# Four channel blocks at a time in the first modulation of a hybrid diffusion layer: weights in 512-channel packets

## The chip, the core and the metric

The kernel runs on one core of one Trainium2 chip. The metric is device time in microseconds (us) of one execution; the median of three executions stands for the kernel, and the range of the three is shown with it. TensorE multiplies matrices; VectorE, ScalarE and GpSimd do elementwise work; SyncE issues most of the transfers from device memory. The profile calls the engines PE (with PEld for its weight loads), DVE, ACT, POOL and SP.

## The reference, cut to what matters

One layer over 512 latent tokens and 256 context tokens, 1024 channels. The part that the change touches is the first of the two adaptive norms:

```python
mod_x = (jax.nn.silu(c) @ w_ada[l] + b_ada[l]).reshape(bsz, N_MOD, 1, D_MODEL)
mod_c = (jax.nn.silu(c_ctx) @ w_ada[l] + b_ada[l]).reshape(N_MOD, D_MODEL)
hc = rms_norm(ctx, norm1_w[l]) * (1.0 + mod_c[1]) + mod_c[0]
hx = rms_norm(x, norm1_w[l]) * (1.0 + mod_x[:, 1]) + mod_x[:, 0]
zs = hn @ w_in[:, :N_STATE_COLS]      # hn is hc, then hx; and so on for the layer
```

Here `mod[0]` is the shift and `mod[1]` the scale, each 1024 channels, and each channel needs a sum over the 1024 entries of `silu(c)`. Everything behind it (two token mixers, their merge, the gated MLP with a 3x3 convolution, the last norm) is unchanged.

## The kernel before

Products keep nearly full float32 precision by splitting each factor into a rounded part ("hi", type fp32r) and a rest ("lo"): `mm3` makes hi·hi, hi·lo and lo·hi. ScalarE makes the hi part with a cast, VectorE or GpSimd the lo part with a subtraction. The order in which each engine's instructions stand is set when the program is built, by a scheduler that places the instructions of the written program by its own reckoning of their times; on the chip each engine then works its list from the top and waits where an operand is not there yet.

The stage in question is `streams`, the first of the kernel. It runs like this:

- `stream_load` brings the six 128-token blocks (two of context, four of latents) as `xn`, 128 x 1024. `stream_in` takes the root mean square (a square on ScalarE, `rpow` with a power on GpSimd), scales `xn` on VectorE, transposes eight 128 x 128 squares on TensorE (`ps_xt`) and copies them to `xT`, half on ScalarE, half on VectorE. So channels lie on partitions.
- `ada_load(k, j)` brings the weights of one block k of 128 channels, for shift (j = 0) or scale (j = 1): 16 tiles `uw`, each 1024 input rows by 128 channels, 512 KB. They share nine buffers with the `xn`.
- `ada_rows(k)` multiplies them: the conditioning vectors (four columns: hi and lo of latent and context) are the stationary operand, the weights the moving one. The six tiles in `UF` go as plain float32, eight products of 128 columns each; the other ten are split into `uh` (ScalarE, two buffers) and `ul` (VectorE, two buffers), sixteen products of 128 columns each. ScalarE copies the four rows out as `adr`.
- `ada_cols(k)` transposes the rows back to channels on partitions (two small transposes), adds bias and parts (`adt`, `mod`) and forms `modA`, the scale of block k.
- `stream_mod(k)` applies `modA` and `modB` to block k of `xT`: `hx` and `hc` (hi, on ScalarE), `hl_t` (VectorE), and the lo parts on VectorE (latents) and GpSimd (context).
- `products(k)` adds block k to four sums: `ps_gc` and `ps_gx` (the gates' weights `wg`) and `pc_k` and `px_k` (the first head's key weights `wk0`), twelve products. Later the first head's `px_q` and `pc_v` follow in the same way.

The loop over k calls `ada_cols(k)`, `stream_mod(k)`, `products(k - 1)` and `ada_rows(k + 2)`: each block of 128 channels has its own small chain from its two weight tiles to its products. The weights `wk0`, `wq0`, `wv0` of the projections are split by `split`, whose subtraction runs on GpSimd in this stage (`sub_eng`).

Of the kernel before, what the change touches and what calls it, by code (L numbers as in the profile page):

```python
# [66 lines left out]
class Kern:  # L67
# [175 lines left out]
        self.modA = cp.tile([P, KC, 2], F32, tag="modA", name="modA")  # L243
        self.modB = self.mod[:, 0:8, :]

    def ada_load(self, k, j, xp):
# [4 lines left out]
        return w

    def ada_rows(self, k, ap):

# [1 line left out]
        ps = self.pt([P, 512], ("mg", "po")[k % 2], f"ps_ada{k}")
        for j in range(2):
            w = self.uw[2 * k + j]
            if (2 * k + j) in UF:
                for i in range(KC):  # L260
                    nc.tensor.matmul(ps[0:4, P * j : P * j + P], self.sc4[:, i, :], w[:, i, :], start=i == 0, stop=i == KC - 1)
                continue
            hi = ap.tile([P, KC, P], F32R, tag="uh", name=f"uh{k}_{j}", bufs=UH)
            lo = ap.tile([P, KC, P], F32R, tag="ul", name=f"ul{k}_{j}", bufs=UH)
# [2 lines left out]
            for p in (hi, lo):
                for i in range(KC):
                    nc.tensor.matmul(ps[0:4, P * j : P * j + P], self.sch[:, i, :], p[:, i, :], start=i == 0 and p is hi, stop=i == KC - 1 and p is lo)
        r = ap.tile([4, 2 * P], F32, tag="adr", name=f"adr{k}", bufs=2)  # L270
        nc.scalar.copy(r, ps[0:4, 0 : 2 * P])
        return ps, r

    def ada_cols(self, k, ps, r, ap):

        nc = self.nc
        for j in range(2):
            nc.tensor.transpose(ps[:, 256 + 4 * j : 260 + 4 * j], r[:, P * j : P * j + P], self.ident[0:4, 0:4])
        t = ap.tile([P, 2, 4], F32, tag="adt", name=f"adt{k}", bufs=2)
        nc.vector.tensor_tensor(t, ps[:, 256:264].rearrange("p (n j) -> p n j", j=4),  # L280
                                self.bada4[:, k : 16 : KC, :], ALU.add)
        m = self.mod[:, k : 16 : KC, :]
        nc.vector.tensor_tensor(m, t[:, :, 0:2], t[:, :, 2:4], ALU.add)
        nc.vector.scalar_tensor_tensor(self.modA[:, k, :], self.mod[:, KC + k, :], 1.0, self.n1w[:, k : k + 1].broadcast_to([P, 2]), ALU.add, ALU.mult)
# [1349 lines left out]
```

## Time and profile before

| | |
|---|---|
| median of 3 runs | 1322.67 us (1321.39 to 1322.98) |
| the profiled execution, its own time | 1323.87 us |
| its span, first to last instruction | 1322.2 us |
| TensorE busy | 1284.0 us, 97% of the span |
| VectorE busy | 888.1 us, 67% |
| ScalarE busy | 585.0 us, 44% |
| GpSimd busy | 531.3 us, 40% |
| mean granted TensorE clock | 0.993 |

All durations below come from the one profiled execution. Its own time is 1.67 us above its span and 1.2 us above the median. A "busy" TensorE counts modelled ends of pipelined products, so what a product costs in a dense run is read from the distance between the starts of neighbours. The stage of the change is the first 70 us of the span.

### The profile page before, as it was taken

The numbers are of one execution on the slowest core, as the hardware profiler recorded it, in microseconds if no ns is written. First come the engines' busy times: TensorE is split into PE (matmuls) and PEld (weight loads), VectorE is DVE, ScalarE is ACT, GpSimd is POOL, SyncE is SP. The second block draws the span as 40 slices with busy tenths as digits, with TensorE's granted clock in tenths as the row PEclk, the third lists the DMA queues.
The fourth block names the chain that finished last, engine by engine and source line by source line (L and its number), as shares of the span: only waits on it lengthen the run. The fifth ranks groups of instructions, "written<-read, shape, count | busy, mean of one in ns | idle before, by whom it ended". The sixth has DMA issues, their size and how long they took to land.

```text
span 1322.2 us, 24197 instructions
## 1 busy us (share of the span) xinstructions
PE 1284.0 (97%) x9454; PEld 1089.1 (82%) x9454; DVE 888.1 (67%) x1809; ACT 585.0 (44%) x1283; POOL 531.3 (40%) x679
## 2 busy tenths in 40 slices
PE   6998899999999999999999999999999999999997
PEld 4886778888888888998899888888788888888886
DVE  6877777857857757253745585444679879887843
ACT  5565664666655744233333354222344333333322
POOL 4313330123122238486847550000445545555542
PEclk9999899999999999999999999999999999999999
DMA  9634233232332244454524433438233333333231
GB/s 282 157 107 117 53 90 101 77 80 77 80 96 68 71 103 134 107 153 107 136 72 128 120 86 92 140 96 253 65 118 90 96 95 98 97 104 98 67 108 68
DMA packets 233248, 141.86 MB, mean 107 GB/s; under 512 B 32992, under 2 KB 215533, under 8 KB 233133
## 3 DMA queue, kind: packets, MB, share of 16 engines
q1 hardware_dynamic: 230973, 140.09, 37.9%
q8 instruction: 74, 1.21, 0.4%
q10 hardware_dynamic: 2160, 0.23, 0.1%
q14 instruction: 41, 0.34, 0.1%
HBM read 134.47 MB, written 5.82 MB: 106 GB/s over the span
## 4 chain that ended last, share of the span: by engine, by line
PE 77%; DVE 6%; ACT 2%; DMA 2%; issue 1%; SPq 0%; POOL 0%; POOLq 0%; ACTq 0%; DVEq 0%
PE pu L124 12%; PE pd L124 6%; PE pu L125 6%; PE py L124 4%; PE px_g L124 4%; PE pv L124 3%; PE pd L125 3%; PE py L125 2%; PE px_g L125 2%; PE px_mo L124 2%; PE po L986 2%; PE pv L125 2%; PE p L1003 2%; PE px_q L124 1%; PE px_z L124 1%; PE px_v L124 1%
## 5 line engine op out<-in xcount | busy, mean ns | idle before, releaser
L1604 DVE SCALAR_TENSOR_TENSOR y<-pu,fw,y 128x441 f32<-128x441 f32 (+2 forms) x352 | 230.0, 690 | 41.1 <-ACT y L1595 35.4
L299 POOL TENSOR_TENSOR aw<-aw,sc 128x512 f32<-128x512 f32 x64 | 70.8, 1109 | 55.8 <-DMA aw<-in_w_ada_dram 55.6
L148 POOL TENSOR_TENSOR rs<-pw_t,mhalf 128x1 f32<-128x1 f32 x14 | 7.9, 563 | 161.8 <-DVE pw_t L147 160.1
L148 POOL TENSOR_TENSOR kh<-pw_t,phalf 128x6 f32<-128x6 f32 x8 | 11.2, 1395 | 129.4 <-DVE pw_t L147 129.4
L302 POOL TENSOR_TENSOR aw<-aw 128x256 f32<-128x256 f32 x64 | 52.4, 822 | 2.9
L857 POOL MEMSET gx<- 96x16 f32 x8 | 1.0, 125 | 114.5 <-DMA gx<-scr 114.5
L1011 ACT ACTIVATE v<-p,sc 128x128 f32<-128x128 f32 x80 | 25.5, 368 | 37.7 <-PE p L1003 37.5
L1533 POOL TENSOR_TENSOR al<-y,ah 128x512 fp32r<-128x512 f32 x22 | 28.6, 1300 | 28.6 <-ACT ah L1532 28.6
L1358 DVE SCALAR_TENSOR_TENSOR x<-x,py 128x512 f32<-128x512 f32 x16 | 11.0, 687 | 41.9 <-PE py L125 41.9
L864 POOL TENSOR_TENSOR gx<-gx,iv_t 96x14 f32<-96x14 f32 (+6 forms) x112 | 34.6, 309 | 8.7
L1595 ACT ACTIVATE y<-pu,fw 128x512 f32<-128x512 f32 x44 | 29.9, 683 | 17.5 <-PE pu L125 16.1
L1161 DVE SCALAR_TENSOR_TENSOR C<-C,ge,mpc 128x257 f32<-128x257 f32 x32 | 15.3, 477 | 32.5 <-PE mpc L1157 32.3
L862 POOL TENSOR_TENSOR iv_t<-gx 96x14 f32<-96x14 f32 (+6 forms) x112 | 33.6, 300 | 8.0
L656 ACT ACTIVATE cv_t<-cv_y 128x512 f32<-128x512 f32 (+1 forms) x40 | 21.7, 543 | 30.2 <-DVE cv_y L655 26.8
L999 DVE SCALAR_TENSOR_TENSOR X<-p,colA,vt 128x128 f32<-128x128 f32 x80 | 24.4, 346 | 12.2 <-PE p L995 11.6
L1532 ACT CAST ah<-y 128x512 fp32r<-128x512 f32 x22 | 13.6, 619 | 40.5 <-DVE y L1531 40.5
L719 DVE SCALAR_TENSOR_TENSOR Eg<-Eg,colA,mask 128x128 f32<-128x128 f32 x96 | 28.2, 353 | 4.4 <-DMA Eg<-gd 4.4
L1022 DVE SCALAR_TENSOR_TENSOR S<-S,ge,p 128x128 f32<-128x128 f32 x64 | 19.2, 342 | 14.5 <-PE p L1015 14.2
L1169 ACT ACTIVATE mn<-mp,colA 128x257 f32<-128x257 f32 x32 | 15.2, 474 | 30.7 <-PE mp L1165 28.7
L1531 DVE TENSOR_TENSOR y<-y,y 128x512 f32<-128x512 f32 x22 | 27.9, 1266 | 0.9
L995 PE MATMUL p<-S,kT 128*128 128x128 f32 x160 | 27.7, 281 | 0.7 <-DVE S L1022 0.5
L1045 POOL TENSOR_TENSOR fo<-fo,mhalf 128x4 f32<-128x4 f32 x8 | 8.5, 1069 | 48.5 <-DVE fo L1044 48.5
(1222 smaller groups left out, 4571.5 us busy)
## 6 DMA issues: line engine op xcount, KB each, us to landing
aw<-in_w_ada_dram SPq DMA_DIRECT2D x64, 256.0 KB
uw<-in_w_ada_dram SPq DMA_DIRECT2D x16, 512.0 KB
Eg<-gd SPq DMA_DIRECT2D x16, 384.0 KB
qs<-gd SPq DMA_DIRECT2D x16, 256.0 KB
xn<-in_x_dram SPq DMA_DIRECT2D x4, 512.0 KB
Em<-r1d SPq DMA_DIRECT2D x8, 256.0 KB
mwo_0r<-in_w_in_dram SPq DMA_DIRECT2D x4, 512.0 KB
mwo_1r<-in_w_in_dram SPq DMA_DIRECT2D x4, 512.0 KB
```

What stands on the lines that cost most here:

```text
L124: for i in (mm(out, lh, rh, start=start, stop=False), mm(out, lh, rl, start=False, stop=False), mm(out, ll, rh, start=False, stop=stop)):
L125: mm(out, ll, rh, start=False, stop=stop)):
L299: g = eng.tensor_tensor(w, w, self.sc[:, 4 * (j % 2) : 4 * (j % 2) + 4, 0:1].broadcast_to([P, 4, P]), ALU.mult)
L302: eng.tensor_tensor(w[:, 0:2, :], w[:, 0:2, :], w[:, 2:4, :], ALU.add)
L719: self.follow(nc.vector.scalar_tensor_tensor(E[:, c, :], E[:, c, :], self.colA[:, c, d, row : row + 1], self.mask[d], ALU.add, ALU.min), "v")
L862: eng.tensor_tensor(t, Bi[:, 0:j, j : j + 1].broadcast_to([8 * NB, j, n]), Bi[:, j : j + 1, j + 1 :].broadcast_to([8 * NB, j, n]), ALU.mult)
L864: g = eng.tensor_tensor(Bi[:, 0:j, j + 1 :], Bi[:, 0:j, j + 1 :], t, ALU.add)
L995: g = nc.tensor.matmul(p1[:, d, :], kT[:, c * P : c * P + P], S[d], start=True, stop=True)
L1531: nc.vector.tensor_tensor(ys[0], ys[0], ys[1], ALU.mult)
L1533: nc.gpsimd.tensor_tensor(al[:, j, :], ys[0], ah[:, j, :].bitcast(F32), ALU.subtract)
L1595: nc.scalar.activation(y, ps, AF.Copy, scale=tap(0, 0))
L1604: g = nc.vector.scalar_tensor_tensor(o, u3[:, r0 + dy : r1 + dy, c0 + dx : c1 + dx], tap(dy, dx), o, ALU.mult, ALU.add)
```

## The change

The same 16 tiles of 512 KB are cut the other way. A tile now holds 256 input rows by 512 channels (`[P, 2, 512]`), so each contiguous piece in memory is 512 channels, 2 KB, where it was 128 channels, 512 B. Number n stands for group g = n // 8 (channels 512 g to 512 g + 511, which are four blocks), row quarter i and shift or scale j. A group's shift and scale are two sums over four tiles each.

- `ada_part(n)` makes a tile's products with 512 columns: two in plain float32 for a tile in `UF`, which is now (0, 1, 15), or two for `uh` and two for `ul`.
- `ada_mods(g)` replaces `ada_cols`: when all eight tiles of a group are in, ScalarE copies the shift rows and VectorE the scale rows out, eight small transposes follow, and one `adt`, one `mod` and one `modA` make four blocks' vectors.
- The loads of tiles 0 to 3 now alternate with the loads of the latents; tiles 0 to 7 (the first group) are worked off during and right after `stream_in`, and the second group's tiles two at a time in the loop over k = 0 to 3, with `ada_mods(1)` at k = 3.

```diff
-UF = (0, 1, 2, 3, 7, 11)
+UF = (0, 1, 15)
...
-        w = xp.tile([P, KC, P], F32, tag="xn", name=f"uw{k}_{j}", bufs=XN)
+        w = xp.tile([P, 2, 512], F32, tag="xn", name=f"uw{n}", bufs=XN)
+        g, i, j = n // 8, n % 8 // 2, n % 2
+        c0 = D * j + 512 * g
...
+        for m, (v, p) in enumerate(parts):
+            for k in range(2):
+                nc.tensor.matmul(ps[0:4, :], v[:, 2 * i + k, :], p[:, k, :], start=i + k + m == 0, stop=i == 3 and k == 1 and m == len(parts) - 1)
...
+        nc.scalar.copy(r[:, 0, :], self.pa[g, 0][0:4, :])
+        nc.vector.tensor_copy(r[:, 1, :], self.pa[g, 1][0:4, :])
+        ps = self.pt([P, 512], ("acc", "mg")[g], f"ps_adt{g}")
...
             for c in range(6):
                 self.stream_in(c, xs[c], xp)
-                if c == 1:
-                    a[0] = self.ada_rows(0, ap)
+                if c > 1:
+                    self.ada_part(c - 2, ap)
             wg = self.gates_weights(xp, ga, gi)
-            a[1] = self.ada_rows(1, ap)
+            for n in range(4, 8):
+                self.ada_part(n, ap)
+            self.ada_mods(0, ap)
...
             for k in range(KC):
-                self.ada_cols(k, *a[k], ap)
                 self.stream_mod(k, xp)
                 if k:
                     products(k - 1)
-                if k + 2 < KC:
-                    a[k + 2] = self.ada_rows(k + 2, ap)
-                if k + 3 == KC:
+                if k < 4:
+                    self.ada_part(8 + 2 * k, ap)
+                    self.ada_part(9 + 2 * k, ap)
+                if k == 3:
+                    self.ada_mods(1, ap)
```

How this moves the instructions shows on three engines. First TensorE, before, at the first modulated product, `ps_gc<-hc0`, which stands between the transposes of the fifth token block (`ps_xt4`):

```order
L358 MATMUL ps_xt2_4_312<-ident_84,xn2_158 128x128 x4
L278 MATMUL ps_ada0_279<-ident_84,adr0_296 128x4 x2
L358 MATMUL ps_xt3_0_326<-ident_84,xn3_160 128x128 x4
L358 MATMUL ps_xt3_4_332<-ident_84,xn3_160 128x128 x4
L261 MATMUL ps_ada1_391<-uw1_0_186,sc4_178 4x128 x8
L358 MATMUL ps_xt4_0_346<-ident_84,xn4_162 128x128 x4
L124 MATMUL ps_gc_236<-hc0_81,wgh_387 128x256
```

And TensorE now, at the same product:

```order
L271 MATMUL ps_ada0_0_299<-ul6_411,sch_179 4x512 x2
L271 MATMUL ps_ada0_1_322<-ul7_419,sch_179 4x512 x2
L283 MATMUL ps_adt0_429<-ident_84,adr0_426 128x4 x8
L271 MATMUL ps_ada1_0_450<-uh8_451,sch_179 4x512 x2
L271 MATMUL ps_ada1_0_450<-ul8_452,sch_179 4x512 x2
L271 MATMUL ps_ada1_1_459<-uh9_460,sch_179 4x512 x2
L271 MATMUL ps_ada1_1_459<-ul9_461,sch_179 4x512 x2
L271 MATMUL ps_ada1_0_450<-uh10_488,sch_179 4x512 x2
L124 MATMUL ps_gc_236<-hc0_81,wgh_390 128x256
```

All 48 transposes of token blocks, all eight tiles of the first group, its eight small transposes and most of three tiles of the second group now stand ahead of that product.

Second VectorE, before, around the first `modA`:

```order
L353 TENSOR_SCALAR xn3_160<-xn3_160,rs3_320 128x1024
L363 COPY xT_141<-ps_xt2_4_312 128x4x128
L280 TENSOR_TENSOR adt0_412<-ps_ada0_279,bada4_181 128x8
L147 SCALAR_TENSOR_TENSOR pw_t_342<-ss4_339,eps_107 128x1
L283 TENSOR_TENSOR mod_184<-adt0_412 128x2x2
L284 SCALAR_TENSOR_TENSOR modA_185<-mod_184,vec_142 128x2
L373 TENSOR_SCALAR hl_t_420<-xT_141,modA_185,mod_184 128x256
```

And VectorE now (`ul2` to `ul5` stand further up):

```order
L372 COPY xT_141<-ps_xt5_4_367 128x4x128
L267 TENSOR_TENSOR ul6_411<-uw6_194,uh6_410 128x1024
L267 TENSOR_TENSOR ul7_419<-uw7_196,uh7_418 128x1024
L278 COPY adr0_426<-ps_ada0_1_322 4x512
L267 TENSOR_TENSOR ul8_452<-uw8_204,uh8_451 128x1024
L290 TENSOR_TENSOR adt0_438<-ps_adt0_429,bada4_185 128x32
L291 TENSOR_TENSOR mod_188<-adt0_438 128x2x8
L267 TENSOR_TENSOR ul9_461<-uw9_206,uh9_460 128x1024
L292 SCALAR_TENSOR_TENSOR modA_189<-mod_188,vec_142 128x8
```

Before, no subtraction `ul` stands ahead of the first `modA`; now eight do, `ul2` to `ul9`.

Third ScalarE now, from the last casts of the first group to the first `hx` and `hc` (before, the first `hc` stands ahead of every `uh`):

```order
L266 CAST uh7_418<-uw7_196 128x1024
L109 CAST wk0h_200<-wk0r_198 128x1024
L277 COPY adr0_426<-ps_ada0_0_299 4x512
L266 CAST uh8_451<-uw8_204 128x1024
L266 CAST uh9_460<-uw9_206 128x1024
L266 CAST uh10_488<-uw10_208 128x1024
L381 ACTIVATE hx0_75<-xT_141,mod_188,modA_189 128x512
L381 ACTIVATE hc0_81<-xT_141,mod_188,modA_189 128x256
```

The cast `wk0h` stands one place behind `uh7` here, so GpSimd's subtraction for `wk0` becomes ready while VectorE has `ul6` and `ul7` to do. From the last third of the first head's `pc_v` products on, all remaining TensorE instructions (7038) stand in the same order in both programs; VectorE's are alike from the copies out of `ps_cols` on.

## Rows read from the trace of the kernel before

**Rows 1.** Page, part 1: busy us (share of span) xinstructions of each engine.
```profile
PE 1284.0 (97%) x9454; PEld 1089.1 (82%) x9454; DVE 888.1 (67%) x1809; ACT 585.0 (44%) x1283; POOL 531.3 (40%) x679
```
**Rows 2.** Stretches of the stage: us, busy us (count) by engine, PEclk, DMA, GB/s.
```profile
36.00:42.00 6.00, 6.00 (x51) 5.06 (x50) 5.93 (x10) 4.78 (x9) 1.59 (x2) 1.00 1.18 296
...
sum 59.61, PE 58.30 PEld 46.90 DVE 43.81 ACT 36.52 POOL 20.64; mean PE 6.48 PEld 5.21 DVE 4.87 ACT 4.06 POOL 2.29
```
**Rows 3.** The same view: token blocks arriving (4 KB pieces), then weight tiles (512 B).
```profile
12.00:14.00 2.00, 2.00 (x12) 1.23 (x11) 0.69 (x2) 1.78 (x2) 0.70 (x1) 1.00 1.04 414
...
24.00:26.00 2.00, 2.00 (x18) 1.44 (x17) 1.02 (x2) 1.84 (x3) 1.23 (x1) 1.00 1.23 294
```
**Rows 4.** Waits from 9.6 to 69.2 us: total us, times, longest.
```profile
ACT uh L265 <- DMA uw<-in_w_ada_dram: 1.9, 2, 1.1
```
**Rows 5.** Timeline, TensorE: start us, us, engine, line, out<-in, shape, count [idle before].
```profile
22.88 0.36 PE L124 MATMUL ps_gc<-hc,wgh 128*128 128x256 f32 x1
...
28.74 0.51 PEld L269 LDWEIGHTS ps_ada<-uh,sch 128*4 128x4 f32 x8
...
32.59 0.20 PEld L278 LDWEIGHTS ps_ada<-ident,adr 4*128 4x128 f32 x2 [0.36 <-issue]
...
33.38 1.62 PEld L261 LDWEIGHTS ps_ada<-uw,sc 128*4 128x4 f32 x16
...
64.87 0.40 PE L124 MATMUL px_q<-hx,wq0h 128*128 128x512 f32 x1
...
65.10 0.28 PE L124 MATMUL ps_gc<-hc,wgh 128*128 128x256 f32 x1
...
65.22 0.28 PE L124 MATMUL pc_k<-hc,wk0h 128*128 128x256 f32 x1
...
69.24 0.14 PEld L206 LDWEIGHTS ps_cols<-ident,rows 89*128 89x128 f32 x1
```
**Rows 6.** Tiles `uw`, `xn`, `hl_t`, `ps_ada`: ns min/median/max, first and last start us.
```profile
L265 ACT CAST uh<-uw x10: 1029/1047/1051, 24.6 to 48.9; 128x1024 fp32r<-128x1024 f32 x10
L266 DVE TENSOR_TENSOR ul<-uw,uh x10: 1208/1216/2591, 25.7 to 50.3; 128x1024 fp32r<-128x1024 f32 x10
...
L353 DVE TENSOR_SCALAR xn<-xn,rs x6: 745/753/1207, 8.8 to 22.3; 128x1024 f32<-128x1024 f32 x6
...
L374 POOL TENSOR_TENSOR hc<-hl_t,hc x8: 729/898/1247, 22.3 to 62.5; 128x256 fp32r<-128x256 f32 x8
L374 DVE TENSOR_TENSOR hx<-hl_t,hx x8: 679/689/1224, 30.4 to 62.0; 128x512 fp32r<-128x512 f32 x8
...
L280 DVE TENSOR_TENSOR adt<-ps_ada,bada x8: 153/156/167, 19.7 to 60.1; 128x8 f32<-128x8 f32 x8
```
**Rows 7.** Groups by form, 0 to 70 us: busy us, mean ns | idle before.
```profile
L363 DVE COPY xT<-ps_xt 128x512 f32<-128x512 f32 x6 | 4.1, 685 | 1.2 <-PE ps_xt L358 1.2
L373 DVE TENSOR_SCALAR hl_t<-xT,modA,mod 128x256 f32<-128x256 f32 x8 | 3.2, 406 | 0.0
...
L372 ACT ACTIVATE hx<-xT,mod,modA 128x512 fp32r<-128x512 f32 x8 | 6.5, 815 | 5.1 <-DVE modA L284 5.1
L372 ACT ACTIVATE hc<-xT,mod,modA 128x256 fp32r<-128x256 f32 x8 | 4.7, 590 | 0.0
```
**Rows 8.** Timeline, VectorE and GpSimd: one engine's long subtraction and the other's next.
```profile
14.45 1.23 DVE L147 SCALAR_TENSOR_TENSOR pw_t<-ss,eps 128x1 f32<-128x1 f32 x1 [1.76 <-ACT junk L351]
...
24.77 2.41 POOL L111 TENSOR_TENSOR wk0l<-wk0r,wk0h 128x1024 fp32r<-128x1024 f32 x1 [1.78 <-ACT wk0h L109]
25.67 2.59 DVE L266 TENSOR_TENSOR ul<-uw,uh 128x1024 fp32r<-128x1024 f32 x1 [0.80 <-ACT uh L265]
...
28.79 0.53 DVE L373 TENSOR_SCALAR hl_t<-xT,modA,mod 128x512 f32<-128x512 f32 x1
```
**Rows 9.** A later pause of TensorE: a stretch with its clock, and the timeline there.
```profile
136.00:140.00 4.00, 1.69 (x56) 1.12 (x56) 3.23 (x9) 2.21 (x10) 0.00 (x0) 0.58 0.01 4
...
139.36 1.48 PE L895 MATMUL w0p<-gx,y 32*32 32x16 f32 x96 [2.31 <-DVE y L890]
```

More of the change, by code (lines that the diff above doesn't have):

```diff
@@ L244, in ada_first, with ada_load @@
         self.modB = self.mod[:, 0:8, :]
-    def ada_load(self, k, j, xp):
-        w = xp.tile([P, KC, P], F32, tag="xn", name=f"uw{k}_{j}", bufs=XN)
-        c0 = D * j + P * k
-        self.anchor["d"] = self.nc.sync.dma_start(w, self.I["w_ada"][0][:, c0 : c0 + P].rearrange("(k p) c -> p k c", p=P))
+    def ada_load(self, n, xp):
+        w = xp.tile([P, 2, 512], F32, tag="xn", name=f"uw{n}", bufs=XN)
+        g, i, j = n // 8, n % 8 // 2, n % 2
+        c0 = D * j + 512 * g
+        self.anchor["d"] = self.nc.sync.dma_start(w, self.I["w_ada"][0][256 * i : 256 * i + 256, c0 : c0 + 512].rearrange("(k p) c -> p k c", p=P))
@@ L251, in ada_load, with ada_part @@
         return w
-    def ada_rows(self, k, ap):
+    def ada_part(self, n, ap):
         nc = self.nc
[L256 to L264, printed above, removed]
+        g, i, j = n // 8, n % 8 // 2, n % 2
+        if i == 0:
+            self.pa[g, j] = self.pt([P, 512], ("acc", ("mg", "po")[j])[g], f"ps_ada{g}_{j}")
+        ps, w = self.pa[g, j], self.uw[n]
+        if n in UF:
+            parts = [(self.sc4, w)]
+        else:
+            hi = ap.tile([P, 2, 512], F32R, tag="uh", name=f"uh{n}", bufs=UH)
+            lo = ap.tile([P, 2, 512], F32R, tag="ul", name=f"ul{n}", bufs=UH)
@@ L265, in ada_rows @@
             self.anchor["u"] = nc.scalar.copy(hi, w)
             nc.vector.tensor_tensor(lo, w, hi.bitcast(F32), ALU.subtract)
[L267 to L274, printed above, removed]
+            parts = [(self.sch, hi), (self.sch, lo)]
@@ L276, in ada_cols, with ada_mods @@
+        for m, (v, p) in enumerate(parts):
+            for k in range(2):
+                nc.tensor.matmul(ps[0:4, :], v[:, 2 * i + k, :], p[:, k, :], start=i + k + m == 0, stop=i == 3 and k == 1 and m == len(parts) - 1)
+    def ada_mods(self, g, ap):
         nc = self.nc
+        r = ap.tile([4, 2, 512], F32, tag="adr", name=f"adr{g}", bufs=1)
+        nc.scalar.copy(r[:, 0, :], self.pa[g, 0][0:4, :])
+        nc.vector.tensor_copy(r[:, 1, :], self.pa[g, 1][0:4, :])
+        ps = self.pt([P, 512], ("acc", "mg")[g], f"ps_adt{g}")
@@ L277, in ada_cols @@
         for j in range(2):
[L278 to L284, printed above, removed]
+            for k in range(4):
+                m = 4 * (4 * j + k)
+                nc.tensor.transpose(ps[:, m : m + 4], r[:, j, P * k : P * k + P], self.ident[0:4, 0:4])
@@ new lines, in ada_mods, with by @@
+        t = ap.tile([P, 2, 4, 4], F32, tag="adt", name=f"adt{g}", bufs=2)
+        b = slice(4 * g, 4 * g + 4)
+        def by(x):
+            return x.rearrange("p (j k) f -> p j k f", j=2)[:, :, b, :]
+        nc.vector.tensor_tensor(t, ps[:, 0:32].rearrange("p (j k f) -> p j k f", j=2, k=4), by(self.bada4), ALU.add)
+        nc.vector.tensor_tensor(by(self.mod), t[:, :, :, 0:2], t[:, :, :, 2:4], ALU.add)
+        nc.vector.scalar_tensor_tensor(self.modA[:, b, :], self.mod[:, KC + 4 * g : KC + 4 * g + 4, :], 1.0,
+                                       self.n1w[:, b].unsqueeze(2).broadcast_to([P, 4, 2]), ALU.add, ALU.mult)
@@ L382, in streams @@
             ga, gi = self.gates_loads()
-            self.uw = [self.ada_load(n // 2, n % 2, xp) for n in range(2)]
-            xs += [self.stream_load(c, xp) for c in range(2, 6)]
+            self.uw, self.pa, self.norms = [], {}, []
+            for c in range(2, 6):
+                self.uw.append(self.ada_load(c - 2, xp))
+                xs.append(self.stream_load(c, xp))
             self.vector_cols(rows, 0)
@@ L387, in streams @@
             self.sub_eng = self.nc.gpsimd
-            self.uw += [self.ada_load(n // 2, n % 2, xp) for n in range(2, 4)]
+            self.uw += [self.ada_load(n, xp) for n in range(4, 8)]
             wk = self.w_cols(self.I["w_in"][0], 1024, "wk0", (self.wraw, xp))
-            self.uw += [self.ada_load(n // 2, n % 2, xp) for n in range(4, 16)]
+            self.uw += [self.ada_load(n, xp) for n in range(8, 16)]
             rows = self.vectors(xp, 1)
```

2 lines of the change are left out of this document (removed).

## The prediction

> **What bounds the kernel now.** I read the engines' shares first: TensorE is busy 97% of the span [rows 1], so time is won only where TensorE has less to do or waits less. The stage table comes next, from 9.63 us, where TensorE starts, to 69.24 us, where the first head's `pc_v` ends [rows 2, 5]. TensorE shows 58.30 of 59.61 us there, but that counts modelled ends. Counted by distances of starts in dense runs the work is smaller, and this is the reckoning that I use. A product of 512 columns costs 0.23 us (64.87 to 65.10), one of 256 columns 0.12 (65.10 to 65.22), a `uh` or `ul` product of 128 columns 0.064 (eight in 0.51), a plain float32 one 0.20 (sixteen records, two to a product, in 1.62), a small transpose 0.10 [rows 5]. The order lists give the counts up to 69.24: `ada` products 160 x 0.064 = 10.2 and 48 x 0.20 = 9.7, small transposes 1.6, block transposes 48 x 0.10 = 4.8 (taken as one float32 record each), products(k) 48 x 0.23 + 48 x 0.12 = 16.8, `px_q` 24 x 0.23 = 5.5, `pc_v` 24 x 0.12 = 2.9. The sum is 51.5 of 59.6 us, so about 8.1 us are waits and a slow start. Transfers are not the bound: ScalarE's casts wait for the tiles `uw` only twice, 1.9 us together [rows 4], though the queue is full. VectorE is nearly full from 36 to 42 us (5.93 of 6) [rows 2], and that is the engine to watch.
>
> **Transfers.** Token blocks in 4 KB pieces came at 414 GB/s, weight tiles in 512 B pieces at 294 [rows 3]. Pieces of 2 KB lie between; I take 350 to 414. Six blocks and eight tiles of 512 KB are 7.3 MB, 18 to 21 us at these rates, so the eighth tile is in by some 20 to 25 us (an estimate; the first us are slower). It is worth nothing in the sum, since the casts hardly waited, and below the first group is paced by VectorE and later than that. Its range goes from a gain of 1.9 us, the whole wait of rows 4, to nothing. [...]
>
> **TensorE's work.** Removed: 10.2 + 9.7 = 19.9 us of `ada` products. Added: 13 split tiles x 4 products = 52 x 0.23 = 12.0, and three plain tiles x 2 products; four times 128 columns gives 4 x 0.20 = 0.8 each, 4.8 together. The 16 small transposes stay. So the stage has 19.9 - 16.8 = 3.1 us less, 48.4 us in all. That is the gain if nothing else changes. The bound below is a rate of the float32 products that does not grow with the columns (another 3.6 us off); the one above is none. I take the sum, as 128 to 512 columns went from 0.064 to 0.23 for the split kind. [...] The rows show 64 and 230 ns, and I keep to them.
>
> **What moves: the first product.** Before, the first product `ps_gc<-hc` starts at 22.88 us [rows 5], since block 0 needs two tiles. Now block 0 needs eight tiles, and the lists show what stands ahead. I follow VectorE. Its list up to the end of the step at 14.45 us is as before, and that step ends at 15.68, held by GpSimd's subtraction [rows 8]. Then until `ul7`: five copies `xT` x 0.685 = 3.4 [rows 7], four scalings x 0.753 = 3.0, six subtractions `ul2` to `ul7` x 1.216 = 7.3 [rows 6], and for the norms' small steps and one wait on GpSimd 1.2 (an estimate: three like `adt` with 0.16, and one round trip to GpSimd). That gives 15.7 + 14.9 = 30.6. In that time GpSimd's `wk0l` becomes ready, since its cast is next behind `uh7`. In rows 8 `wk0l` takes 2.41 us, and the `ul` issued during it took 2.59 instead of 1.22: it ended 1.08 us after GpSimd did. So I add 2.4, giving 33.0. Then the last tile's two products, 0.46, and hand-overs, 0.2; the copy of four rows by 512, which no row shows and which lies between 0 and the 0.685 of a 512-column copy, taken as 0.685; `ul8`, 1.22, during which the transposes run; `adt` and `mod`, 0.16 each; `ul9`, 1.22; `modA`, 0.16: 37.3. ScalarE makes `hx` 0.815 and `hc` 0.590 [rows 7]: **first product at 38.7 us**, 15.8 later than before. ScalarE's three casts ahead of `hx` lie under this, as `uh10` waits for `ul8`'s buffer users and ends near 36.8.
>
> **What is left then, and what waits.** TensorE has by then done its block transposes, 17 of the 26 halves of split tiles (two products each), two plain tiles and eight small transposes: 4.8 + 17 x 0.46 + 3.2 + 0.8 = 16.6 us. Left: 48.4 - 16.6 = 31.8 us. With no more waits the stage ends at 70.5. But the second group is a second barrier. From 37.3 VectorE has four blocks of `hl_t` (0.53 + 0.406) and `hx` lo (0.689), 6.5 us [rows 6 to 8], `ul10` to `ul14`, 6.1, and four of GpSimd's `hc` subtractions of about 0.75 that it does not overlap with (their least is 0.729), 3.0: it ends at 52.9. Behind `ul13`, at 51.7, TensorE goes on at 52.2 with its products done; its work up to there is four blocks of products, 8.4, and eight halves, 3.7, through at 50.8, so it waits 1.4. Then come `uw15`, `ul14`, GpSimd's `wq0l` (about 2.4, as `wk0l`), `px_q`, the second transposes and `modA`; `px_q` and `pc_v` fill most of it. I leave 0.4 us open there and 1.0 for the first `hx` lo of block 4, which needs `hl_t` three times and a subtraction behind `modA`, about 2.2, against 1.1 us of products that need none. So the end is 70.5 + 1.4 + 1.4 = 73.3 against 69.24: **+4.1 us**. From there TensorE's list is the same and dense, so the shift goes through to the end. The profiled execution, 1323.87, would become 1328.0; the median of the runs shown is 1.2 us lower, so the forecast is 1322.67 + 4.1 = 1326.8 us.
>
> **The rivals.** (a) No change: GpSimd and VectorE do not hold each other up as rows 8 suggest, or the held time falls where VectorE waits anyway. Then 2.4 us go ahead of the first product and 3.0 in the second group: the first product comes at 36.3, the wait of 1.4 is gone, and the stage ends at 36.3 + 31.8 + 1.4 = 69.5, so 1322.9. For it: VectorE is idle for 15.8 us of the stage [rows 2]. Against it: rows 8. [...] (c) Faster: VectorE starts on the first group earlier than I add. Its place is VectorE ahead of 15.68 us: the step at 14.45 had waited 1.76 us and was held 1.1 more [rows 8]. If the casts and subtractions get those 2.8 us and `wk0l` does not hold them (2.4), the first product comes at 33.5, the waits of the second group but for 0.4 hide behind TensorE's work, and the end is 33.5 + 31.8 + 0.4 = 65.7: -3.5, 1319.2. It decides from a first product before about 34.4 us. Against it: the list puts `ul2` behind the scalings of two further blocks, which follow that step.
>
> **How the numbers follow.** A measurement of this kernel tells about 0.2%, 2.6 us, from no change. Forecast 0.57 (its own range 1324.5 to 1329), rival (a) 0.25, (b) 0.11, (c) 0.07. Of the forecast's chance 0.03 lies within 0.2%, of (a)'s 0.01 above it: slower 0.57 - 0.03 + 0.11 + 0.01 = 0.66, same 0.27, faster 0.07. The range leaves out (c), the lowest part of (a) and the worst of (b): 1321.5 to 1331. It takes in most of the transfers' 1.9 us below and of the clock's 4 us above.
>
> **What would show it.** [...] I am wrong if TensorE is dense between 23 and 39 us, if the stage ends within 2 us of 69.24, or if a later stage takes the shift back.

## The result, and the profile after

| | median us | runs | profiled execution | its span | mean granted clock |
|---|---|---|---|---|---|
| kernel before | 1322.03 (1319.64 to 1322.98) | 4 | 1323.87 | 1322.2 | 0.993 |
| changed kernel | 1328.54 (1327.73 to 1329.49) | 4 | 1329.49 | 1327.8 | 0.990 |

The ratio is 1.0058 (95% interval 1.0043 to 1.0073). That is +7.7 us; the two medians differ by 6.5 us (their quotient is 1.0049). Forecast were 1326.8 and +4.1. The sign, the range and the rough size came out. The main cause did not, and most of what follows is about that.

The page's first line for TensorE and its row of granted clock by 40 slices, for the changed kernel, answer to [rows 1]:

```profile
PE 1285.1 (97%) x9262; PEld 1079.2 (81%) x9262; DVE 886.3 (67%) x1796; ACT 585.1 (44%) x1280; POOL 534.5 (40%) x679
PEclk8999999999999999999999999999999999999999
```

TensorE is as full as before; its first slice is new, with a clock under 0.9. The timeline of TensorE in the changed kernel (start us, us, engine, line, operation, shape, count, idle time before it and what ended that) answers to [rows 5]:

```profile
11.77 2.60 PE L271 MATMUL ps_ada<-uw,sc 128*4 128x512 f32 x4
17.73 1.94 PE L367 MATMUL ps_xt<-ident,xn 128*128 128x128 f32 x8 [3.36 <-DVE xn L362]
19.60 3.58 PE L271 MATMUL ps_ada<-uw,sc 128*4 128x512 f32 x4
...
41.87 0.39 PE L124 MATMUL ps_gc<-hc,wgh 128*128 128x256 f32 x1 [0.33 <-ACT hc L381]
44.82 0.39 PE L124 MATMUL ps_gc<-hc,wgh 128*128 128x256 f32 x1 [1.97 <-POOL hc L383]
...
61.86 0.65 PE L283 MATMUL ps_adt<-ident,adr 4*128 4x4 f32 x8
64.06 0.51 PE L124 MATMUL ps_gx<-hx,wgh 128*128 128x512 f32 x1 [0.16 <-ACT hx L381]
...
76.79 0.24 PE L206 MATMUL ps_cols<-ident,rows 89*128 89x89 f32 x1
```

The first product stands at 41.87 us (22.88 before, 38.7 forecast). The stage ends at 76.79, where the transposes `ps_cols` start (69.34 before, 73.3 forecast; the forecast counted from 69.24, where that product's weight load starts), so the change costs 7.45 us there; the two profiled spans differ by 5.6. The stretches of the changed kernel (busy us and counts by engine, granted clock, DMA share, GB/s) answer to [rows 2, 3]:

```profile
10.00:16.00 6.00, 4.37 (x12) 1.75 (x12) 0.34 (x4) 0.59 (x1) 0.00 (x0) 1.00 1.06 388
16.00:18.00 2.00, 0.27 (x2) 0.30 (x3) 1.33 (x7) 0.12 (x1) 0.55 (x1) 0.67 0.77 216
18.00:20.00 2.00, 2.00 (x9) 1.34 (x8) 0.39 (x1) 2.00 (x4) 1.00 (x1) 0.50 0.92 360
20.00:22.00 2.00, 2.00 (x3) 0.26 (x2) 1.97 (x2) 2.00 (x4) 1.83 (x2) 0.50 0.51 130
22.00:24.00 2.00, 2.00 (x9) 0.89 (x8) 1.16 (x3) 0.46 (x2) 0.63 (x2) 0.63 0.36 138
32.00:40.00 8.00, 5.98 (x28) 1.60 (x25) 7.24 (x9) 6.24 (x7) 2.99 (x1) 1.00 1.05 391
41.87:76.79 34.92, 32.78 (x175) 24.60 (x176) 18.49 (x30) 17.00 (x25) 16.23 (x10) 1.00 0.24 62
```

Three things stand out. From 10 to 16 us the queue moves 388 GB/s, but VectorE does 0.34 us of work and GpSimd none. From 20 to 24 us the transfers fall to 130 to 138 GB/s. And TensorE's granted clock is 0.50 from 18 to 22 us, behind the pause that ended at 17.73. What VectorE stood at, in its timeline of the changed kernel:

```profile
9.06 0.75 DVE L362 TENSOR_SCALAR xn<-xn,rs 128x1024 f32<-128x1024 f32 x1 [0.67 <-POOL rs L148]
15.66 0.18 DVE L456 COPY oTg<-gx 128x32 f32<-128x32 f32 x1 [5.84 <-DMA gx<-in_w_in_dram]
...
16.83 0.75 DVE L362 TENSOR_SCALAR xn<-xn,rs 128x1024 f32<-128x1024 f32 x1 [0.67 <-POOL rs L148]
...
20.01 1.37 DVE L147 SCALAR_TENSOR_TENSOR pw_t<-ss,eps 128x1 f32<-128x1 f32 x1 [1.62 <-ACT junk L360]
...
36.93 2.02 DVE L267 TENSOR_TENSOR ul<-uw,uh 128x1024 fp32r<-128x1024 f32 x1
...
40.32 0.16 DVE L292 SCALAR_TENSOR_TENSOR modA<-mod,vec 128x8 f32<-128x8 f32 x1
```

`gx` here is the gate weights' second small load, 64-byte pieces on ScalarE's queue, issued at 2.24 us in this kernel and at 2.25 before. The changed lines do not touch it. Before, it held VectorE for 0.39 us, and the copy ran at 9.96; now it holds it for 5.84 us, to 15.66. Behind that copy, in VectorE's order, stand the scaling of `xn1` and everything else, so the step that stood at 14.45 [rows 8], `pw2` in the expectations below, stands at 20.01. SyncE waited too (issues of its queue in the changed kernel: start us, us that they took, count; then from its table of waits up to 30 us: total us, times, longest):

```profile
8.39 0.54 SPq L251 DMA_DIRECT2D uw<-in_w_ada_dram  x1
15.73 0.33 SPq L351 DMA_DIRECT2D xn<-in_x_dram  x1
16.16 8.61 SPq L251 DMA_DIRECT2D uw<-in_w_ada_dram  x4
...
SPq L351 <- DMA gx<-in_w_in_dram: 6.7, 1, 6.7
SPq L251 <- PE ps_xt L367: 4.5, 4, 2.1
SPq L251 <- PE ps_ada L271: 3.0, 1, 3.0
```

Nothing was issued between 8.93 and 15.73: by the table of waits SyncE's queue stood 6.7 us for `gx`, and then 4.5 and 3.0 us for buffers that TensorE's late transposes and products had to free first. Hence the 130 GB/s.

Why was it late? The DMA queues in the first us, packets, MB and share of the 16 engines. The kernel before, 6 to 8 us (q1 is SyncE's queue, q10 ScalarE's):

```profile
q1 hardware_dynamic: 589, 0.34, 75.7%
q10 hardware_dynamic: 1327, 0.11, 55.2%
```

The changed kernel, 6 to 8 us and then 8 to 10 us:

```profile
q1 hardware_dynamic: 263, 0.54, 83.5%
q10 hardware_dynamic: 809, 0.07, 31.2%
...
q1 hardware_dynamic: 258, 0.72, 93.7%
q10 hardware_dynamic: 250, 0.02, 9.1%
```

SyncE's queue sends 589 packets in 2 us before, 1327 small ones beside them; now 263, and 809 small ones, then 258 and 250. From 6 to 8 us SyncE's packets average 2.1 KB in the changed kernel (0.54 MB in 263) and 0.58 KB before (0.34 MB in 589); beside the larger ones 809 small packets got through in those 2 us, beside the smaller ones 1327. How the 16 engines choose between the two queues these counts do not show.

### The profile page after: what moved, and what is told of

Read it like the earlier page. It is cut to its first block, busy times and chain, and to the rows that moved or that the text cites. A ratio compares the mean times of both kernels' runs of the same rounds, so it can differ in the third digit from the quotient of the medians.

```text
span 1327.8 us, 23796 instructions
## 1 busy us (share of the span) xinstructions
PE 1285.1 (97%) x9262; PEld 1079.2 (81%) x9262; DVE 886.3 (67%) x1796; ACT 585.1 (44%) x1280; POOL 534.5 (40%) x679
## 4 chain that ended last, share of the span: by engine, by line
PE 77%; DVE 6%; DMA 2%; ACT 2%; issue 1%; SPq 0%; POOL 0%; POOLq 0%; ACTq 0%; DVEq 0%
PE pu L124 12%; PE pd L124 6%; PE pu L125 6%; PE py L124 4%; PE px_g L124 4%; PE pv L124 3%; PE pd L125 3%; PE py L125 2%; PE px_g L125 2%; PE po L998 2%; PE px_mo L124 2%; PE p L1015 2%; PE pv L125 2%; PE px_q L124 2%; PE px_z L124 1%; PE px_v L124 1%
## 5 line engine op out<-in xcount | busy, mean ns | idle before, releaser
L1543 DVE TENSOR_TENSOR y<-y,y 128x512 f32<-128x512 f32 x22 | 32.5, 1477 | 0.9
```

Source lines behind the costliest of these rows:

```text
L1543: nc.vector.tensor_tensor(ys[0], ys[0], ys[1], ALU.mult)
```

## The experiments

Theory A: the late gate load costs the 7 us. Theory B, which is the prediction's own: the barrier of four blocks (no product before all eight tiles of a group are in) costs them, by VectorE's long list. All runs in one table, places in us from the one profiled execution of each kernel; "step" is the end of the norm step that stood at 14.45 before, the point from which the prediction counted VectorE's list.

| kernel | gx copied at | step ends | first product | stage ends | from first product | median us | ratio to before (95%) |
|---|---|---|---|---|---|---|---|
| before | 9.96 | 15.68 | 22.88 | 69.34 | | | 1 |
| changed | 15.66 | 21.38 | 41.87 | 76.79 | 34.92 | 1328.54 | 1.0058 (1.0043 to 1.0073) |
| e1_gates_sync | 8.22 | 13.57 | 34.72 | 69.63 | 34.91 | 1321.34 | 0.9998 (0.9986 to 1.001) |
| e2_before_gates_sync | 8.24 | 15.91 | 22.17 | 70.32 | | 1318.75 | 0.998 (0.9967 to 0.9992) |
| e4_groups_128 | 11.06 | 16.78 | 39.08 | 73.96 | 34.88 | 1326.91 | 1.0035 (1.0022 to 1.0048) |
| e5_small_pieces | 9.88 | 15.59 | 36.29 | 71.22 | 34.93 | 1324.94 | 1.003 (1.0014 to 1.0047) |
| e6_gates_late | 26.41 | 13.72 | 42.53 | 77.67 | 35.14 | 1332.72 | 1.0074 (1.0052 to 1.0097) |
| e6b_gates_behind_xn2 | 16.40 | 13.87 | 39.54 | 74.11 | 34.57 | 1327.36 | 1.0041 (1.0026 to 1.0056) |
| e7_before_late_gates | 15.97 | 13.50 | 22.61 | 74.43 | | 1323.8 | 1.0015 (0.9998 to 1.0032) |
| e3_plain_first | 8.11 | 13.47 | 36.01 | 70.57 | 34.56 | 1322.45 | 1.0006 (0.9991 to 1.0022) |
| e9_second_only_sync | 8.19 | 15.17 | 21.45 | 68.82 | | 1319.74 | 0.9984 (0.9968 to 1.0) |

In every kernel with a group of four blocks first, the stage ends 34.6 to 35.1 us behind the first product. So the first product is the one number to explain in the stage. The time follows the stage's end less closely: the kernel before had a median of 1321.49 us beside e1, e2, e4 and e6, 1320.46 beside e5, e6b, e7 and e9, and 1320.48 beside e3, and against these the times lie up to 4 us from what the stage's end gives (e2: 1.0 us later at the stage's end, 2.7 us faster).

**The gate load in time.**

```
-        nc.scalar.dma_start(ga, ...)
-        nc.scalar.dma_start(gi, ...)
+        nc.sync.dma_start(ga, ...)
+        nc.sync.dma_start(gi, ...)
```

> Edit: the changed kernel with the two small loads of the gate weights issued on SyncE's queue instead of ScalarE's, so that they stand in order behind xn1 and ahead of the first 512-channel weight tile. Theory A (the late gate load): in the changed kernel these small loads landed at about 15.6 us instead of 9.9, VectorE stood before the copy out of gx for 5.8 us, and its whole list started 5.7 us late. By A gx lands between 8 and 11 us, the step pw2 (20.01 in the changed kernel) starts near 15, the first ps_gc product (41.87) stands near 36.5 to 37.5, ps_cols (76.79) near 71.5 to 73, and the time is 1323.5 to 1325.5. Theory B (the barrier of four blocks sets it, the 5.8 us lie beside other waits): the first product stays at 41 to 42.5 and the time at 1328 to 1329.

VectorE and TensorE of this kernel:

```profile
8.22 0.17 DVE L456 COPY oTg<-gx 128x32 f32<-128x32 f32 x1
...
13.07 0.50 DVE L147 SCALAR_TENSOR_TENSOR pw_t<-ss,eps 128x1 f32<-128x1 f32 x1 [2.29 <-ACT junk L360]
...
34.72 0.39 PE L124 MATMUL ps_gc<-hc,wgh 128*128 128x256 f32 x1 [0.33 <-ACT hc L381]
...
69.63 0.24 PE L206 MATMUL ps_cols<-ident,rows 89*128 89x89 f32 x1
```

The first product came 7.15 us earlier than in the changed kernel, more than A said, and the time fell by some 7 us, to that of the kernel before (below A's range, too). A had counted VectorE's wait alone; here SyncE's queue has no long wait for `gx` either (its issues from 6.41 to 10.42 us follow each other within 0.22 us), and TensorE's clock stays at 1.00 from 18 to 24 us. B falls as the main cause of the loss: with the barrier in place and the load in time, the stage ends 0.3 us from where it ended before. The same two lines in the kernel before are the control.

> Edit: the same move of the gate weights' two small loads to SyncE's queue, made in the kernel before (control). There gx landed at 9.96 and held VectorE for 0.39 us only. By A nothing is to be won: the first product stays within 1 us of 22.88 and the time within 2 us of the kernel before (1320 to 1324). Were the move worth something by itself (less work on ScalarE's queue, another order of the transfers), it would show here as much as in the changed kernel: 3 us or more.

The stage ends at 70.32, 1 us later than before, yet the time is 2.7 us lower (0.998), so the move gains a little here too, just above what I allowed. It is not won in this stage; see the clock, below. Against this kernel, the changed one with its load moved is 2.6 us slower (1321.34 to 1318.75). So of the loss, 4 to 5 us are the late load by this control, and 2.6 us are left that it does not explain.

**Large packets or the other order of loads?** Two kernels ask what made the load late. The first has the groups without the wide tiles:

```
-        w = xp.tile([P, 2, 512], F32, tag="xn", name=f"uw{n}", bufs=XN)
-        c0 = D * j + 512 * g
+        w = xp.tile([P, KC, P], F32, tag="xn", name=f"uw{n}", bufs=XN)
+        c0 = D * j + 512 * g + P * i
...
-            for k in range(2):
-                nc.tensor.matmul(ps[0:4, :], ...)
+            for k in range(KC):
+                nc.tensor.matmul(ps[0:4, P * i : P * i + P], ...)
```

> Edit: the changed kernel with its groups of four blocks, its order of loads and its one chain for each group left, but tiles and products of 128 channels as in the kernel before (512-byte pieces, 128-column products into a quarter of the accumulator). It has the barrier without the wide packets; TensorE has 3.1 us more products. Theory A: with 512-byte pieces on SyncE's queue the small gate load on the other queue lands at 9 to 11 us again, VectorE's list starts 4 to 6 us earlier than in the changed kernel, the first product stands at 36 to 39, and the time is 1324 to 1327.5 although TensorE's products are the longer ones. Theory B: gx matters nothing, the first product stays at 41 to 43 (the transfers are slower besides) and the time is 1330 to 1333.

`gx` landed early enough to be copied at 11.06 (a wait of 1.56 us), as A said. The first product only came at 39.08, just outside A's range (36 to 39), the time inside it: its list is 1.2 us later at the step, a `ul` waited 1.67 us for ScalarE's cast (its tiles came at 293 GB/s from 24 to 30 us), and the clock was at 0.50 from 36 to 38 us. The second kernel changes the pieces of the first four tiles alone:

```
+        for c in range(0, 512, P if n < 4 else 512):
+            e = P if n < 4 else 512
-        ...dma_start(w, ...[256 * i : 256 * i + 256, c0 : c0 + 512]...)
+            ...dma_start(w[:, :, c : c + e], ...[256 * i : 256 * i + 256, c0 + c : c0 + c + e]...)
```

> Edit: the changed kernel with its first four weight tiles loaded as four transfers of 128 channels each, in pieces of 512 bytes, into the same tiles; products, splits, groups and the queue of the gate loads stay. It tells what made the gate load late. Theory A1 (size of the pieces that SyncE's queue moves beside it): gx lands at 9 to 11.5 us instead of 15.6, as in the kernel before (9.9) and with 128-channel tiles (11.0); the first product then stands at 35.5 to 39 instead of 41.9, and the time is 1322 to 1326.5, the upper end if the slower transfers hold the splits. Theory A2 (the order of the loads, two weight tiles more ahead of the gates' turn): gx lands at 14 to 16.5 us all the same, the first product stays at 41 to 44, time 1328 to 1331.

VectorE of this kernel, and its queues from 6 to 8 us:

```profile
9.88 0.17 DVE L458 COPY oTg<-gx 128x32 f32<-128x32 f32 x1
...
14.22 1.37 DVE L147 SCALAR_TENSOR_TENSOR pw_t<-ss,eps 128x1 f32<-128x1 f32 x1 [1.50 <-ACT junk L362]
...
31.35 2.02 DVE L269 TENSOR_TENSOR ul<-uw,uh 128x1024 fp32r<-128x1024 f32 x1
```

```profile
q1 hardware_dynamic: 591, 0.33, 72.8%
q10 hardware_dynamic: 1404, 0.11, 57.9%
```

With the same order of loads, tiles, products and splits, pieces of 512 bytes give the small load its 1404 packets back, and VectorE does not wait for it at all. A1 holds: the piece size beside it made the load late; the order alone does not. But this kernel, with the load in time and the barrier in place, is still 1.003 (1.0014 to 1.0047) of the kernel before, some 4 us slower.

**VectorE's wait or SyncE's?** The load stays late, and its copies are moved down VectorE's order, behind the scaling of block 5 (`norms[5]`) and, in the second kernel, of block 2 (`norms[2]`):

```
-            nc.vector.tensor_copy(wg[:, :, 72 + 32 * d : 76 + 32 * d], gi[:, :, 4 * d : 4 * d + 4])
-            nc.vector.tensor_copy(wg[:, :, 32 * d + 8 : 32 * d + 12], gi[:, :, 8 + 4 * d : 12 + 4 * d])
+            for o, s in ((72, 0), (8, 8)):
+                g = nc.vector.tensor_copy(wg[:, :, o + 32 * d : o + 4 + 32 * d], gi[:, :, s + 4 * d : s + 4 + 4 * d])
+                self.queue_after(g, self.norms[5])
```

> Edit: the changed kernel with the four small copies out of gx put behind the last scaling of xn in VectorE's order; the loads stay on ScalarE's queue and land as late as they do (15 to 16 us). It takes away the wait on VectorE alone; the wait that SyncE's queue has for the same load (6.7 us in the changed kernel) stays. Theory A, if VectorE's order is the whole path: pw2 starts near 15, first product 36.5 to 38, time 1323.5 to 1325.5. If SyncE's queue matters as well, xn2 and the tiles behind it land late all the same: first product 38.5 to 41, time 1325.5 to 1328. Theory B: first product 41 to 42.5, time 1328 to 1329.

The first product came at 42.53, where B has it within 0.1 us, but for another reason; the time, 1332.72, is above every case of the expectation. GpSimd and VectorE of this kernel:

```profile
28.13 3.23 POOL L111 TENSOR_TENSOR wgl<-oTg,wgh 128x1024 fp32r<-128x1024 f32 x1 [2.42 <-ACT wgh L109]
31.45 3.25 POOL L111 TENSOR_TENSOR wk0l<-wk0r,wk0h 128x1024 fp32r<-128x1024 f32 x1
...
29.62 6.16 DVE L267 TENSOR_TENSOR ul<-uw,uh 128x1024 fp32r<-128x1024 f32 x2
```

The step ended at 13.72, so the wait on VectorE was gone. The late copies then made GpSimd's split of the gate weights late, right against that of `wk0`, and two subtractions of VectorE beside them took 6.16 us instead of 2.35. TensorE's clock then fell, too: it was 0.83 from 30 to 36 us and 0.60 from 36 to 42. The run moved the cost and told nothing on A, so the second kernel puts the copies earlier.

> Edit: the changed kernel with the four copies out of gx put behind the scaling of xn2 in VectorE's order; the loads stay where they are and land at 15 to 16.5 us. With the copies behind xn5 VectorE no longer stood before gx, but the splits of the gate weights and of wk0 came together on GpSimd (28.1 to 34.7 us), two subtractions on VectorE beside them took 6.16 us instead of 2.35, and the time rose to 1332.7. Here the copies come early enough that the gates' split lies well ahead of wk0's. If VectorE's wait is the whole cost: pw2 near 13.6, first product 35 to 37.5, time 1322 to 1325. If SyncE's queue, which waits for the same load, matters as well (123 GB/s from 16 to 18 us with the copies behind xn5): xn3 is late as there (its square starts near 17.6), first product 37.5 to 40.5, time 1324.5 to 1327.5. If neither matters: 41 to 43 and 1328 or more.

VectorE, SyncE's queue and two stretches of this kernel:

```profile
16.40 0.44 DVE L457 COPY oTg<-gx 128x32 f32<-128x32 f32 x4 [1.04 <-DMA gx<-in_w_in_dram]
...
16.46 0.33 SPq L351 DMA_DIRECT2D xn<-in_x_dram  x1
...
16.00:18.00 2.00, 2.00 (x11) 1.04 (x11) 1.10 (x5) 1.10 (x2) 0.00 (x0) 1.00 0.65 142
36.00:40.00 4.00, 3.68 (x10) 1.53 (x11) 3.93 (x9) 3.22 (x5) 0.79 (x1) 0.57 0.49 164
```

VectorE waits 1.04 us instead of 5.84, and the first product comes 2.3 us earlier than in the changed kernel; the stretch behind `gx` still runs at 142 GB/s. By its numbers this is the middle case of the expectation, in which both waits count; that SyncE's wait costs something by itself is not shown by it. Of the 7.15 us that the moved load gives back, 2.3 came with VectorE's order alone. The other 4.8 are SyncE's starved queue together with two things of this kernel: a `ul` held by GpSimd (2.74 us at 20.78, 1.5 over its usual) and a clock of 0.57 from 36 to 40 us. I could not part these further.

**A late load without the change.** In the kernel before, the gate loads go to SyncE's queue behind `xn3` (`nc.scalar.dma_start` becomes `nc.sync.dma_start`, as above):

```
-            ga, gi = self.gates_loads()
             self.uw = [self.ada_load(n // 2, n % 2, xp) for n in range(2)]
-            xs += [self.stream_load(c, xp) for c in range(2, 6)]
+            xs += [self.stream_load(c, xp) for c in range(2, 4)]
+            ga, gi = self.gates_loads()
+            xs += [self.stream_load(c, xp) for c in range(4, 6)]
```

> Edit: the kernel before, everything of its modulation left, but the gate weights' two small loads put on SyncE's queue behind xn3, so that they land late (14 to 17 us instead of 9.9) without any 512-channel packet. Theory A: VectorE stands before the copy out of gx for 3 to 6 us and TensorE, which has 58.3 us of work in the 59.6 us of the stage, loses most of it: first product 26 to 29 instead of 22.9, ps_cols 72 to 75 instead of 69.2, time 1324.5 to 1328. Theory B (the late load lies beside other waits): first product 22 to 25, ps_cols 69 to 71, time 1319 to 1323.

The premise failed: the copies came late (15.97), but the order of this kernel had put them behind two scalings, so VectorE waited for nothing there, and the first product stayed at 22.61. The stage still ended 5 us late, and the time was some 2 to 3 us longer, between the two theories, with an interval that still holds no change. GpSimd, VectorE and TensorE of this kernel, for the longest wait of its stage:

```profile
52.40 2.74 POOL L111 TENSOR_TENSOR wq0l<-wq0r,wq0h 128x1024 fp32r<-128x1024 f32 x1 [3.42 <-ACT wq0h L109]
55.09 2.34 POOL L111 TENSOR_TENSOR wv0l<-wv0r,wv0h 128x1024 fp32r<-128x1024 f32 x1
...
52.80 2.35 DVE L283 TENSOR_TENSOR mod<-adt 128x4 f32<-128x4 f32 x1
55.19 2.26 DVE L284 SCALAR_TENSOR_TENSOR modA<-mod,vec 128x2 f32<-128x2 f32 x1
...
58.35 0.50 PE L124 MATMUL ps_gx<-hx,wgh 128*128 128x512 f32 x1 [2.36 <-ACT hx L372]
```

Two steps of VectorE on 4 and 2 elements per partition, 0.15 to 0.18 us in the kernel before from 19.88 to 35.05 us, took 2.35 and 2.26 us, each ending with GpSimd's long subtraction. TensorE stood 2.36 us for them, and its clock then fell (0.71 from 58 to 62 us). The rest of the 5 us I did not trace.

**What sets the first product once the load is in time.** The gate loads are on SyncE's queue as in e1, and:

```
-UF = (0, 1, 15)
+UF = (0, 1, 2, 3, 4, 5, 15)
```

> Edit: the changed kernel with the gate loads on SyncE's queue (first product at 34.7 us, ps_cols at 69.6, 1321.34 us) and, besides, weight tiles 2 to 5 of the first group taken unsplit: four subtractions of 1.22 us fewer on VectorE (4.9 us), four conversions fewer on ScalarE, and on TensorE for each of the four tiles 1.81 us of unsplit products in place of 0.92 us, 3.6 us more in all. It asks what sets the first product once the gate load is in time. Theory V (VectorE's list, as the prediction had it): the first product stands 3 to 5 us earlier, at 29.7 to 31.7; the work behind it, 34.9 us in both kernels so far, is the same, so ps_cols is at 64.6 to 66.6 and the time 1316.5 to 1319. Theory T (TensorE's products of the first group, or the arrival of the tiles, hold it as well): the first product stays at 33 to 36, ps_cols at 68 to 71, time 1320 to 1323.

Stretches of TensorE's first group in this kernel, and one wait of VectorE:

```profile
9.00:20.00 11.00, 10.82 (x43) 4.14 (x42) 6.52 (x13) 6.97 (x12) 4.01 (x4) 1.00 1.03 401
20.00:30.00 10.00, 9.10 (x37) 2.96 (x35) 4.96 (x7) 5.88 (x9) 1.43 (x2) 1.00 1.07 370
...
22.45 0.69 DVE L372 COPY xT<-ps_xt 128x512 f32<-128x512 f32 x1 [1.45 <-PE ps_xt L367]
```

Theory T holds. VectorE's work in 20 to 30 us fell to 4.96 us (9.24 with the splits left in), but now VectorE waits for TensorE, which is busy 19.92 of 21 us with the unsplit products. The first product came 1.3 us later than in e1, not 3 to 5 earlier. Some 0.4 us of that can be the clock, which fell here (0.83 from 30 to 40 us, 0.77 from 34 to 38) and not in e1 (1.00 from 30 to 40): `modA` is 0.9 us later than in e1, the first product 1.3. In e1 TensorE is busy 18.38 of the same 21 us, so four tiles moved from VectorE to TensorE are too many; whether one or two would win was not tried.

**Half of the change.** Blocks 0 to 3 with a vector each and tiles of 128 channels, blocks 4 to 7 as one group, gate loads on SyncE's queue, `UF = (0, 1, 2, 3, 7, 15)`:

```
+        if n < 8:
+            w = xp.tile([P, KC, P], F32, tag="xn", name=f"uw{n}", bufs=XN)
+            ...
...
+                if k < 4:
+                    self.ada_cols(k, *a[k], ap)
...
+                if k < 2:
+                    a[k + 2] = self.ada_rows(k + 2, ap)
```

> Edit: blocks 0 to 3 as in the kernel before (tiles of 128 channels, a vector for each block), blocks 4 to 7 as in the changed kernel (512-channel packets, one chain), and the gate loads on SyncE's queue. It keeps the half of the change that has no first product to wait for it. Theory A: the first barrier is all that the change costs once gx lands in time, and the second half saves 1.5 us of TensorE's products: first product near 22.2, ps_cols 68.3 to 70, time 1317 to 1319.5 (the kernel before with the same move of the gate loads took 1318.75). Rival: the second barrier makes TensorE wait 1 to 2 us near 50 to 55 us, which takes the saving back: ps_cols 70 to 72, time 1319 to 1321.

The stage ends at 68.82, the earliest of all, 1.5 us ahead of the kernel before with the same move, as A had it for the stage. Its median, 1319.74, is not in A's range (1317 to 1319.5) but in the rival's. As a ratio it is 0.9984 (up to 1.0) beside 0.998 for e2: no difference shown. These two are the fastest kernels of the study; what they win comes with the moved load, and the wide packets add nothing that can be measured.

**The clock.** Part of what the stage doesn't explain goes with TensorE's mean granted clock. The runs sorted by it, mean us and number of runs:

| clock | before (with e1, e2) | e1 | e2 | e9 | changed |
|---|---|---|---|---|---|
| 0.990 | 1325.4 (1) | | | | 1329.5 (1) |
| 0.991 | 1325.5 (1) | | | | |
| 0.992 | 1324.1 (3) | 1322.6 (3) | | | 1328.3 (3) |
| 0.993 | 1323.2 (4) | 1323.3 (2) | | 1321.1 (2) | |
| 0.994 | 1320.9 (11) | 1321.2 (6) | 1320.4 (3) | 1320.3 (6) | |
| 0.995 | 1320.8 (7) | | 1319.2 (4) | 1318.3 (3) | |
| 0.996 | 1320.2 (2) | 1319.2 (1) | 1317.7 (3) | 1317.3 (1) | |
| 0.997 | | | 1317.6 (2) | | |

At 0.994 the kernel before, e1, e2 and e9 lie within 0.9 us; at 0.995 and 0.996, with few runs, they lie up to 2.9 us apart, so the clock is not all of it. In the kernel before, 0.992 to 0.996 are 3.9 us, some 1 us for each 0.001. The mean clock is 0.9935 in e1 and 0.9953 in e2, so about 1.8 of the 2.6 us between them go with the clock (an estimate from these numbers). The changed kernel is 4.2 us slower than the kernel before at the same 0.992. Why the clock falls more often in one than in the other I did not find.

## Why the prediction was right and wrong

**The bound.** TensorE at 97%, and the time decided by when the dense work of this stage starts: right. The first product alone places the stage's end (34.6 to 35.1 us behind it, in seven kernels); the time it places only within some 4 us.

**Transfers.** The rate, 350 to 414 GB/s: right, 388 and 391. "It is worth nothing in the sum" is the step that failed. I looked at who waits for the large tiles, and not at who shares the DMA engines with them. Pieces of 512 bytes came at 291 GB/s (the kernel before, 20 to 22 us) and pieces of 2 KB at 391 (the changed kernel, 32 to 40 us).

**VectorE's list.** "Its list up to the end of the step at 14.45 us is as before" was wrong by 5.7 us (21.38 instead of 15.68). In the order it is indeed as before; in time it hung on a load that the change does not name, and the 0.39 us that VectorE waited for this load before was the warning. From that step on the list was shorter than I made it, 20.5 us instead of 23.0, by about 1.6 in one term: the `ul` beside `wk0l` took 2.02 us in place of 1.22, and I had added 2.4, since the first 2 us of GpSimd's 2.99 fell on a `ul` that was under way, a wait, and a copy out of the accumulator. The remaining 0.9 is spread over many steps. Sum: +5.7 - 2.5 = +3.2, 41.87 instead of 38.7.

**Rival (a) came closer in the stage.** In e5_small_pieces the step ends at 15.59, as the prediction assumed, and the first product stands at 36.29; rival (a) said 36.3. That they agree so well is luck in part: (a) puts the hold between GpSimd and VectorE at nothing, and the `ul` beside `wk0l` was held 0.8 us in e5, too (2.02 us). The stage of e5 then ends at 71.22, 1.9 us late, where the forecast had 4.1 and (a) had 0.3. With the load still earlier (e1) the price is 0.3 us. So at the stage's end the barrier, for which I forecast the loss, costs 0.3 to 1.9 us. In time it is less clear: e1 is no slower than the kernel before but 2.6 us slower than e2, and e5 is 4.0 us slower (1.8 to 6.2), as much as I had forecast. The barrier's share of the loss thus lies between 0 and about 4 us and stays open; the late load, which I had not seen, has the rest, 4 to 7 us. The number came out within the range because that load took the place of what the barrier costs less than forecast. That is luck: the sign rested mainly on the wrong cause.

**TensorE's work, and what is left.** 34.6 forecast, 34.92 measured, with other parts: 32.78 busy (31.8 forecast) and 2.14 idle. Unsplit wide products cost 1.81 us a tile (from 13.84 to the next work at 15.65 in e3), 1.6 forecast. The wait before the second group, 1.4 + 1.4 us, was 0.16; in its place TensorE stood 1.97 us at 44.82 for GpSimd's `hc` subtraction, which took 2.87 us beside VectorE.

**Rival (b), the clock.** Its fall of the clock between 30 and 45 us, with 2 to 4 us of the dense work lost, and the 4 us that the range leaves for the clock were the author's estimates: in the kernel before the clock is 1.00 from 9.63 to 69.24 us, and in the changed kernel it was 1.00 from 30 to 42 us, so the rival's place was wrong. But it fell at about 16.7 us (0.82 from 16.50 to 16.75, 0.54 from 16.50 to 24 us), within TensorE's pause of 3.36 us that ended at 17.73, and in four of the variants (e3, e4, e6, e6b) it fell between 30 and 42 us, about where the rival had it, though mostly ahead of the first product: 0.83 over ten microseconds in e3, 0.57 over four in e6b, 0.72 over six in e4, 0.72 over twelve in e6. That is 1.7 us at most in e3, e4 and e6b, 3.4 in e6, and 3.5 in the changed kernel at its earlier place; none reaches the 4 us.

**Through to the end.** "The shift goes through": 7.45 us at the stage's end, 5.6 at the end of the profiled spans, 6.5 in the medians. On the way it was not constant. TensorE's products stand in the same order from `ps_cols` on, so each can be compared with its own start in the kernel before: in the changed kernel they are 7.4 us late at 75 us, 8.5 behind `ps_gr` at 80.6, 10.0 at 112, 5.5 at 140, 7.2 at 188 and 5.4 at the end. The 1.1 us at `ps_gr`, the gates' transposes, come in all seven kernels with a group of four blocks first and not in e2 or e7; in the changed kernel TensorE stands 0.94 us there for VectorE. So the change also costs something behind its stage, which the prediction had put at nothing. The fall from 10.0 to 5.5 is no gain of the change: nine of the ten other traces gain 3.8 to 5.2 us on this one trace of the kernel before from 120 to 140 us, so that execution of it was slow there. The clock's falls stand elsewhere as well: from 137 to 144 us it was 0.54 before and 1.00 now; from 112 to 116, 146 to 150 and 184 to 188 us it was 1.00 before and 0.57, 0.57 and 0.58 now. Which of these falls belongs to the change I can't say.

## What to carry to other kernels

When a transfer is made larger or faster, list every small transfer in flight beside it on any queue, and who waits for it in order: a load of 64-byte pieces fell 5.7 us behind when the pieces beside it grew from 512 to 2048 bytes (its copy ran at 15.66 us instead of 9.96). In the changed kernel the copy that waited for it held all that stood behind it on VectorE, 5.84 us, and SyncE's queue stood 6.7 us for the same load; the cure was to put the small load in the large ones' own queue, ahead of them (in e1 its copy ran at 8.22). After a blind forecast comes true, still test its cause: here the forecast mechanism cost 0 to 4 us of the 7, and a load that the change does not name cost the rest. And compare the end of the whole run, over many runs, with the end of the stage in one trace: here they differed by up to 4 us.
